# Feed-forward products by Strassen's scheme over 2x2 blocks, with the down product as a stage of its own

## The chip, the cores and the metric

The kernel runs on one core of a Trainium2 chip. A core has five engines with an instruction queue each: TensorE (PE in the profile, with its weight loads as PEld), VectorE (DVE), ScalarE (ACT), GpSimd (POOL) and SyncE (SP), which here issues most of the transfers between DRAM and the on-chip memory SBUF. Matrix products end in PSUM banks of 128 partitions by 512 fp32 values; there are eight of them. The metric is the time of one execution on the device in microseconds. The kernel before took 3261.09 us, the median of three runs (3260.57 to 3262.5).

## What is computed

One encoder block over 2048 tokens of width 1024, in fp32. The feed-forward part, which the change is about, has a hidden layer of 2816.

```
for l in range(DEPTH):                        # DEPTH = 1
    h = _rmsnorm(x, norm1_g[l])
    proj = h @ w_in[l]                        # 1024 -> 3264
    ...
    y_a = _hgrn2_group(...)                   # gated linear recurrence, both directions
    y_b = _mla_group(...)                     # latent attention, 4 heads
    x = x + jnp.concatenate([y_a, y_b], axis=-1) @ w_out[l]
    h = _rmsnorm(x, norm2_g[l])
    x = x + (jax.nn.silu(h @ w_gate[l]) * (h @ w_up[l])) @ w_down[l]   # 1024 -> 2816 -> 1024
return _rmsnorm(x, final_norm_g)
```

## The kernel before

Every product keeps fp32 accuracy by a split: an operand is cast to a rounded type on ScalarE (its high part, names ending in h), the rest is subtracted on VectorE or GpSimd (its low part, l), and three matmuls are added in PSUM, high by high, high by low and low by high. That is `mm3`, the lines 192 to 194. So a 128x512 piece of a product over 128 rows of the inner dimension costs three matmuls.

Phases 1 to 3 (input projection with the recurrence, latent projections, attention) are the same in both kernels. Phase 4, the output projection, goes over 16 token tiles of 128: products by `w_out`, the residual, a store of the result to DRAM (`x2_d`), and in `norm2_tile` the second norm, transposed by TensorE and moved out of PSUM. For the first eight tiles it is split in place; for the others it is stored in DRAM (`h2_d`).

Phase 5, the feed-forward part, goes over two halves of 1024 tokens (`hf`) and in each over 22 hidden tiles of 128 (`f`). Per hidden tile: `gate_up` for two blocks of 512 tokens (`bb`), 8 inner tiles x 3 matmuls for gate and as many for up, 96 in all. Then `s`, ScalarE's silu of the gate bank times the up bank on VectorE (L1121), and its split `th` (L1123, ScalarE) and `tl` (L1125, VectorE). `down` multiplies them by one 128x1024 tile of `w_down`, 8 token tiles x 2 column halves x 3 matmuls, 48, and VectorE adds each bank to the accumulator `acc` (L1088). So a hidden tile has 144 matmuls, and the eight banks are four for gate and up and four for down. The weights (`gr`, `ur`, `dr`) are loaded by SP a hidden tile ahead, cast by ScalarE (L989) and their low part is made by GpSimd (L991). At the change of half `h2_load` brings in the other 1024 tokens (L1062, L1063), and the first eight token tiles get their final norm: a sum of squares, a chain of some twelve VectorE operations on one column (`rstd_of`, names `rf_`), and the scaling by the row norm and the gain `gfin` (L1098 on VectorE, L1101 and L1102 on ScalarE and GpSimd). At the end the last two hidden tiles are taken together.

The order of each engine's queue is worked out when the program is built, from the data dependences and the buffers of each pool. So the order of the rows below says what stands behind what on an engine, and not when it runs.

## Time and profile before

| | |
|---|---|
| time, median of 3 runs | 3261.09 us (3260.57 to 3262.5) |
| span of the profiled execution | 3256.8 us (4.3 us below that median) |
| TensorE busy | 3134.8 us, 96%, 17169 matmuls recorded |
| VectorE busy | 1880.0 us, 58% |
| ScalarE busy | 1089.6 us, 33% |
| GpSimd busy | 689.7 us, 21% |
| output projection, inner stretch | 1580 to 1772 us |
| feed-forward part, first to last matmul | 1762.4 to 3245.3 us |

The profile is of one execution. Busy time of TensorE counts overlapping matmuls once, so that it can be near 100% while the engine is not at its best pace. The table by stretches gives the busy time of each engine between two moments, and the granted clock of TensorE in that stretch as a share of its full speed.

### The profile page before, as it was taken

To read this page: it belongs to the slowest core of one execution; us is meant where nothing else is said; L and a number is where in the kernel's file an instruction comes from. 1 tells how busy PE (TensorE), PEld (TensorE's weight loads), DVE (VectorE), ACT (ScalarE), POOL (GpSimd) and SP (SyncE) were. 2 spreads that over 40 slices of the span, in tenths; PEclk is the share of its full clock that TensorE was granted. 3 is DMA by queue.
4 is the path that set the end of the run, shared out by engine and by line. 5 is a ranking of instruction groups with operands and counts; after the bars stand their busy time and mean duration, and the time that the engine had idled before them with its cause. 6 is when DMAs were issued, how large, how long until landed. Compare 5 with 4: busy or idle time off the path is not lost.

```text
span 3256.8 us, 44545 instructions
## 1 busy us (share of the span) xinstructions
PE 3134.8 (96%) x17169; PEld 2628.2 (81%) x17169; DVE 1880.0 (58%) x4276; ACT 1089.6 (33%) x2037; POOL 689.7 (21%) x600
## 2 busy tenths in 40 slices
PE   7999999998989999999999999999999999999998
PEld 6999777776778888888888887888887788787877
DVE  6126558777768888888886434343436543434344
ACT  5101466665225555555432211111114111111112
POOL 1100233232241212110011322222222222212221
...
GB/s 172 71 63 56 64 67 79 75 88 123 198 189 34 40 32 46 24 25 24 167 142 192 87 46 47 45 52 45 52 46 138 107 47 46 46 46 52 46 39 52
DMA packets 231012, 245.00 MB, mean 75 GB/s; under 512 B 13416, under 2 KB 181904, under 8 KB 230800
## 3 DMA queue, kind: packets, MB, share of 16 engines
...
q10 hardware_dynamic: 1088, 2.90, 0.3%
...
q14 instruction: 77, 0.63, 0.1%
...
## 4 chain that ended last, share of the span: by engine, by line
PE 65%; DVE 10%; DMA 1%; issue 1%; ACT 1%; POOL 0%; SPq 0%; DVEq 0%; ACTq 0%; POOLq 0%
PE pu L194 5%; PE pg L193 5%; PE pu L193 5%; PE pu L192 5%; PE pg L192 5%; PE pg L194 5%; PE pd L192 3%; PE t L884 3%; PE pd L193 3%; PE pd L194 3%; DVE acc L1088 3%; DVE tl L1125 2%; PE s L847 2%; PE s L848 2%; PE o L193 2%; PE o L194 2%
## 5 line engine op out<-in xcount | busy, mean ns | idle before, releaser
L1121 DVE TENSOR_TENSOR s<-s,pu 128x512 f32<-128x512 f32 x88 | 60.5, 688 | 791.5 <-PE pu L194 791.5
L1088 DVE TENSOR_TENSOR acc<-acc,pd 128x512 f32<-128x512 f32 x688 | 429.4, 677 | 3.3 <-PE pd L194 3.0
L192 PE MATMUL pd<-dh,th 128*128 128x512 f32 x704 | 280.0, 398 | 29.9 <-DVE acc L1088 27.2
L193 PE MATMUL pd<-dl,th 128*128 128x512 f32 x704 | 275.1, 391 | 0.0
L194 PE MATMUL pd<-dh,tl 128*128 128x512 f32 x704 | 274.9, 391 | 0.0
L192 PE MATMUL pu<-h2h,uh 128*128 128x512 f32 x704 | 274.1, 389 | 0.0
L194 PE MATMUL pu<-h2h,ul 128*128 128x512 f32 x704 | 273.9, 389 | 0.0
L194 PE MATMUL pg<-h2h,gl 128*128 128x512 f32 x704 | 273.9, 389 | 0.0
L193 PE MATMUL pu<-h2l,uh 128*128 128x512 f32 x704 | 273.9, 389 | 0.0
L192 PE MATMUL pg<-h2h,gh 128*128 128x512 f32 x704 | 273.9, 389 | 0.0
L193 PE MATMUL pg<-h2l,gh 128*128 128x512 f32 x704 | 273.9, 389 | 0.0
L197 ACT ACTIVATE pth<-t 128x512 fp32r<-128x512 f32 x256 | 153.8, 603 | 248.0 <-PE t L884 248.0
L991 POOL TENSOR_TENSOR gl<-gr,gh 128x1024 fp32r<-128x1024 f32 x44 | 105.2, 2392 | 573.7 <-ACT gh L989 545.0
L858 DVE TENSOR_REDUCE mx<-s 128x1 f32<-128x512 f32 x256 | 175.3, 686 | 54.8 <-PE s L851 54.8
L991 POOL TENSOR_TENSOR dl<-dr,dh 128x1024 fp32r<-128x1024 f32 x44 | 105.6, 2400 | 423.5 <-ACT dh L989 387.5
L192 PEld LDWEIGHTS pd<-dh,th 128*128 128x128 f32 x704 | 132.5, 188 | 76.8 <-DVE acc L1088 48.9
L989 ACT ACTIVATE dh<-dr 128x1024 fp32r<-128x1024 f32 x44 | 46.7, 1062 | 419.3 <-PE pd L194 413.5
L867 ACT ACTIVATE pr<-s,nb 128x512 f32<-128x512 f32 x256 | 172.8, 688 | 14.9 <-DVE nb L861 11.1
L198 DVE TENSOR_TENSOR ptl<-t,pth 128x512 fp32r<-128x512 f32 x256 | 175.0, 685 | 2.2 <-ACT pth L197 0.5
L192 PE MATMUL o<-pth,vh 128*128 128x256 f32 x512 | 164.2, 321 | 0.3 <-DVE nb L861 0.3
L884 PE MATMUL t<-ident,pr 128*128 128x128 f32 x1024 | 153.2, 272 | 4.3 <-DVE pr L874 3.0
L884 PEld LDWEIGHTS t<-ident,pr 128*128 128x128 f32 x1024 | 125.5, 139 | 37.6 <-issue 1.7
...
## 6 DMA issues: line engine op xcount, KB each, us to landing
...
```

Of the source, the lines that this page charges most:

```text
L192: PE.matmul(ps, a_hi, b_hi, start=first, stop=False)
L193: PE.matmul(ps, a_hi, b_lo, start=False, stop=False)
L194: PE.matmul(ps, a_lo, b_hi, start=False, stop=last)
L197: ACT.activation(hi, ps, AF.Copy)
L198: DVE.tensor_tensor(lo, ps, fr(hi), op=ALU.subtract)
L847: PE.matmul(ps, q_hi[:, qs], k_hi, start=True, stop=False)
L848: PE.matmul(ps, q_hi[:, qs], k_lo, start=False, stop=False)
L858: last_mx[0] = DVE.tensor_reduce(mx[:, b:b + 1], ps, op=ALU.max, axis=AX.X)
L867: ACT.activation(PR[i][:, b, :], SB[i][b], AF.Exp, scale=SCALE, bias=nb, accum_out=rs[:, b:b + 1])
L884: PE.transpose(ps[:, j, :], PR[i][:, b, j * P:(j + 1) * P], ident)
L991: POOL.tensor_tensor(wl, raw, fr(wh), op=ALU.subtract)
L1088: DVE.tensor_add(acc[t][:, ns], acc[t][:, ns], banks[i, n])
```

## The change

The three products of the feed-forward part are made with Strassen's scheme (Winograd's form) over 2x2 blocks: seven products of quarter blocks instead of eight, and additions around them. The seven products are called P1 to P7. For an operand in blocks A11, A12, A21, A22 and weights B11 to B22:

```
S1 = A21+A22  S2 = S1-A11   S3 = A11-A21  S4 = A12-S2
T1 = B12-B11  T2 = B22-T1   T3 = B22-B12  T4' = B21-T2
P1 = A11 B11  P2 = A12 B21  P3 = S4 B22   P4 = A22 T4'  P5 = S1 T1  P6 = S2 T2  P7 = S3 T3
U2 = P1+P6    U3 = P1+P6+P7
C11 = P1+P2   C12 = U2+P5+P3   C21 = U3+P4   C22 = U3+P5
```

For gate and up the two weight matrices stand side by side: the columns 1 are gate, the columns 2 up, the rows 1 and 2 the upper and lower 512 of the inner dimension; the rows of A are two blocks of 512 tokens. A group is one hidden tile of one half of the tokens, 44 groups, in the order of `seq`; each has 7 products of 4 inner tiles x 3 matmuls, 84. P1 and P2 share a PSUM bank (a), P6, P7 and P4 another (b), P5 and P3 a third (c), and a bank is read between the products that go into it. The products of neighbouring groups are interleaved (`prods`, with an offset in groups).

What it adds and moves, part by part:

- *Output projection.* `norm2_tile` no longer splits; it keeps the transposed tiles (`hs`), makes S1 to S4 on GpSimd for every second block of four tiles and stores all seven operands to DRAM.
- *First operands.* `op_load` loads an operand in four pieces through eight raw buffers, casts on ScalarE, makes the low part on VectorE.
- *Gate and up.* `r_load` loads four quarter weights a group ahead, `t_make` makes T1 to T4 on GpSimd, `b_make` casts and makes the low part five products ahead, on VectorE for P2 and P4 and on GpSimd for the others. `after` adds up and multiplies on VectorE, makes the four sums of the down operand there and stores seven operands to DRAM (`g_d`).
- *Change of half.* In the last group of the first half each product is followed by the load of its operand for the second half.
- *Down.* It begins when gate and up are done for all tokens. Six passes P1, P2, P6, P7, P4, P5 have 11 steps of one pair of hidden tiles each, with 8 banks (8 token tiles) x 3 matmuls, 24 a step. A step's operand is loaded from DRAM and split (`g_op`), and its weights are loaded, summed on GpSimd and split (`w_op`: the T sums are made again here, up to three operations on GpSimd, with six raw buffers `wr`), two steps ahead. The banks are added into `t1`, `c11`, `U2` and `U3` after a pass; the residual comes in through `x2r` and a GpSimd addition after P6 and P7. P3 goes over token tiles (`last_g`), 33 matmuls each, so that the final norm of one lies beside the products of the next.

The diff, cut to its core:

```diff
@@ mm3
+    def mm3(ps, a_hi, a_lo, b_hi, b_lo, first, last, more=False):
@@ phase 4 and gate and up
+    OPS = ("A11", "S2", "A12", "S1", "S3", "A22", "S4")
+    def op_load(hf, i, pl):
+        hi, lo = (pl.tile([P, 4, 512], F32R, tag=f"{i}{c}", name=f"{i}{c}_{hf}") for c in "hl")
+        for j in range(4):
+            raw = fwr.tile([P, 512], F32, tag="raw", name=f"opr_{hf}_{i}_{j}", bufs=8)
+            SP.dma_start(out=raw, in_=h2_d[hf][i][:, j, :])
+            ACT.activation(hi[:, j, :], raw, AF.Copy)
+            DVE.tensor_tensor(lo[:, j, :], raw, fr(hi[:, j, :]), op=ALU.subtract)
+        op[i] = (hi, lo)
+    prods = (("P1", 0), ("P4", 1), ("P6", 0), ("P3", 1), ("P2", 0), ("P5", 0), ("P7", 0))
+    def t_make(n):
+        for nm, a, b in (("T1", "B12", "B11"), ("T2", "B22", "T1"), ("T3", "B22", "B12"), ("T4", "B21", "T2")):
...
+            POOL.tensor_tensor(R[nm, n], R[a, n], R[b, n], op=ALU.subtract)
+    def b_make(m):
...
+        pl, tag, bufs = (fwr, "u", 3) if m % 7 < 3 else (fwB, "v", 4)
+        hi, lo = (pl.tile([P, 4, P], F32R, tag=f"{tag}{c}", name=f"{nm}{c}_{n}", bufs=bufs) for c in "hl")
+        ACT.activation(hi, raw, AF.Copy)
+        eng = DVE if pr in ("P2", "P4") else POOL
+        eng.tensor_tensor(lo, raw, fr(hi), op=ALU.subtract)
+    def product(m):
+        if AHEAD > 0:
+            b_make(m + AHEAD)
...
+        for k in range(4):
+            mm3(ps, bh[:, k, :], bl[:, k, :], ah[:, k, :], al[:, k, :], new and k == 0, k == 3, not new)
...
+        if n == NF - 1:
+            op_load(1, A_OF[pr], opA if A_OF[pr] in ("A11", "S2") else fwB)
@@ norm2_tile
+                POOL.tensor_tensor(s1, a21, a22, op=ALU.add)
+                SP.dma_start(out=d["S1"][:, :, o], in_=s1)
+                POOL.tensor_tensor(a21, a11, a21, op=ALU.subtract)
...
@@ after P4
+            DVE.tensor_add(t1, t1, bank["b", n])
+            ACT.activation(t1, t1, AF.Silu)
+            g = G[2, up] = tmp("g", f"2_{n}", 6)
+            DVE.tensor_mul(g, t1, M["U3", n])
@@ down
+    def wd(nm, fp):
...
+        raw = fs.tile([P, 512], F32, tag="wr", name=f"{nm}d", bufs=6)
+        SP.dma_start(out=raw, in_=w_down[0, f * P:(f + 1) * P, n * 512:n * 512 + 512])
+    def w_op(pr, fp, pl, tag, bufs):
...
+        elif nm == "T4":
+            POOL.tensor_tensor(raw, raw, parts_[1], op=ALU.subtract)
+            POOL.tensor_tensor(raw, raw, parts_[2], op=ALU.add)
+            POOL.tensor_tensor(raw, raw, parts_[3], op=ALU.subtract)
...
+        ACT.activation(hi, raw, AF.Copy)
+        DVE.tensor_tensor(lo, raw, fr(hi), op=ALU.subtract)
+    def residual(dst, i, h, n):
+        raw = fd.tile([P, 512], F32, tag="x2r", name=f"x2r_{i}_{h}{n}", bufs=3)
...
+        POOL.tensor_tensor(dst, dst, raw, op=ALU.add)
+    dn = [(pr, fp) for pr in ("P1", "P2", "P6", "P7", "P4", "P5") for fp in range(NP)]
+    for m, (pr, fp) in enumerate(dn):
+        d_make(m + 2)
...
+            mm3(banks[i], th[:, o], tl[:, o], wh, wl, new and fp == 0, fp == NP - 1, not new)
+            if fp == NP - 1:
+                down_after(pr, i, banks[i])
+    LW = [w_op("P3", fp, lw, f"l{fp}", 1) for fp in range(NP)]
...
+            raw = fs.tile([P, NP, P], F32, tag="lr", name=f"lr_{i}", bufs=2)
+            SP.dma_start(out=raw, in_=g_d["S4"][:, :, i * P:(i + 1) * P])
...
-    def down(hf, f0, f1, tiles):
-        banks = {(i, n): bank4(f"pd_{hf}_{f1}_{i}_{n}", "x") for i in tiles for n in range(2)}
...
-                mm3(ps, th[:, o], tl[:, o], wh[:, ns], wl[:, ns], f == f0, f == f1)
...
-                DVE.tensor_add(acc[t][:, ns], acc[t][:, ns], banks[i, n])
```

Three places of the built programs show what stands behind what. The first is TensorE's queue, in the middle of the feed-forward part. Before, where the up product of hidden tile 18 (`pu_0_18_1`) ends and its down product (`pd`, by token tile and column half) begins:

```order
L192 MATMUL pu_0_18_1_22687<-h2h1_17259,uh_0_18_22507 128x512
L193 MATMUL pu_0_18_1_22687<-h2l1_17260,uh_0_18_22507 128x512
L194 MATMUL pu_0_18_1_22687<-h2h1_17259,ul_0_18_22509 128x512
L192 MATMUL pd_0_18_0_0_22727<-dh_0_18_22511,th_0_18_0_22654 128x512
L193 MATMUL pd_0_18_0_0_22727<-dl_0_18_22513,th_0_18_0_22654 128x512
L194 MATMUL pd_0_18_0_0_22727<-dh_0_18_22511,tl_0_18_0_22656 128x512
L192 MATMUL pd_0_18_0_1_22728<-dh_0_18_22511,th_0_18_0_22654 128x512
L193 MATMUL pd_0_18_0_1_22728<-dl_0_18_22513,th_0_18_0_22654 128x512
L194 MATMUL pd_0_18_0_1_22728<-dh_0_18_22511,tl_0_18_0_22656 128x512
```

Now, where P4 of group 1 (operand A22, weights T4, bank `pb_1`) is followed by P6 of group 2 (operand S2, weights T2, bank `pb_2`):

```order
L193 MATMUL pb_1_19175<-A22h_0_18992,T4h_1_19190 128x512
L194 MATMUL pb_1_19175<-A22l_0_18993,T4h_1_19190 128x512
L195 MATMUL pb_1_19175<-A22h_0_18992,T4l_1_19191 128x512
L193 MATMUL pb_2_19323<-S2h_0_18441,T2h_2_19210 128x512
L194 MATMUL pb_2_19323<-S2l_0_18442,T2h_2_19210 128x512
L195 MATMUL pb_2_19323<-S2h_0_18441,T2l_2_19211 128x512
```

The shape of a matmul is the same, 128x512; the down product has left this part, and the products of neighbouring groups alternate. TensorE's list has 14738 rows before and 13946 now, 792 fewer.

The second is GpSimd's queue. Before, in the second half, it holds the low parts of the weights of hidden tiles 10 and 11 and nothing else:

```order
L991 TENSOR_TENSOR gl_1_10_25659<-gr_1_10_25594,gh_1_10_25657 128x1024
L991 TENSOR_TENSOR ul_1_10_25720<-ur_1_10_25596,uh_1_10_25718 128x1024
L991 TENSOR_TENSOR dl_1_10_25724<-dr_1_10_25598,dh_1_10_25722 128x1024
L991 TENSOR_TENSOR gl_1_11_25871<-gr_1_11_25806,gh_1_11_25869 128x1024
L991 TENSOR_TENSOR ul_1_11_25932<-ur_1_11_25808,uh_1_11_25930 128x1024
```

Now, at the passage from P7 to P4 of the down stage, the sums of T4 (`B21d`, three operations for each step) and the residual additions that follow P7 (L1245, into `U3d` and `t1d`):

```order
L1220 TENSOR_TENSOR B21d_27800<-B21d_27800,B11d_27806 128x512
L1245 TENSOR_TENSOR U3d_0_27664<-U3d_0_27664,x2r_0_11_27666 128x512
L1245 TENSOR_TENSOR t1d_0_26247<-t1d_0_26247,x2r_0_10_27669 128x512
L1218 TENSOR_TENSOR B21d_27845<-B21d_27845,B22d_27847 128x512
L1219 TENSOR_TENSOR B21d_27845<-B21d_27845,B12d_27849 128x512
L1245 TENSOR_TENSOR U3d_1_27675<-U3d_1_27675,x2r_1_11_27677 128x512
L1245 TENSOR_TENSOR t1d_1_26254<-t1d_1_26254,x2r_1_10_27680 128x512
L1245 TENSOR_TENSOR U3d_2_27686<-U3d_2_27686,x2r_2_11_27688 128x512
L1245 TENSOR_TENSOR t1d_2_26261<-t1d_2_26261,x2r_2_10_27691 128x512
L1245 TENSOR_TENSOR U3d_3_27697<-U3d_3_27697,x2r_3_11_27699 128x512
L1245 TENSOR_TENSOR t1d_3_26268<-t1d_3_26268,x2r_3_10_27702 128x512
L1220 TENSOR_TENSOR B21d_27845<-B21d_27845,B11d_27851 128x512
```

The sums of the fifth step of P4 (`B21d_27845`) stand among the 16 residual additions, of which eight more follow before the sixth step's sums.

The third is VectorE's queue. Before, in the middle of the first half: the silu products `s`, the low parts `tl` and the additions that clear the banks of `down`:

```order
L1088 TENSOR_TENSOR acc_7_18827<-acc_7_18827,pd_0_7_7_1_20466 128x512
L1121 TENSOR_TENSOR s_0_8_0_20531<-s_0_8_0_20531,pu_0_8_0_20506 128x512
L1125 TENSOR_TENSOR tl_0_8_0_20536<-s_0_8_0_20531,th_0_8_0_20534 128x512
L1121 TENSOR_TENSOR s_0_8_1_20592<-s_0_8_1_20592,pu_0_8_1_20567 128x512
L1088 TENSOR_TENSOR acc_0_18813<-acc_0_18813,pd_0_8_0_0_20607 128x512
L1088 TENSOR_TENSOR acc_0_18813<-acc_0_18813,pd_0_8_0_1_20608 128x512
L1125 TENSOR_TENSOR tl_0_8_1_20597<-s_0_8_1_20592,th_0_8_1_20595 128x512
```

Now, at the passage from P5 to P3, among the row norms of the token tiles that P5 finishes (`rf_13` to `rf_15`, one column each; L1262 is the scaling), the low parts of the first two operands of P3 (`lgl_0` and `lgl_1`, L1332):

```order
L1262 SCALAR_TENSOR_TENSOR t1d_5_26282<-t1d_5_26282,rf_13_r_28781,gfin_25838 128x512
L177 SCALAR_TENSOR_TENSOR rf_14_t_28807<-rf_14_r_28806,rf_14_a_28804 128x1
L184 TENSOR_TENSOR rf_15_r_28831<-rf_15_r_28831,rf_15_t_28832 128x1
L1332 TENSOR_TENSOR lgl_0_28920<-lr_0_28917,lgh_0_28919 128x1408
L186 TENSOR_SCALAR rf_14_a_28804<-rf_14_t_28807 128x1
L177 SCALAR_TENSOR_TENSOR rf_15_t_28832<-rf_15_r_28831,rf_15_a_28829 128x1
L187 TENSOR_TENSOR rf_14_t_28807<-rf_14_a_28804,rf_14_t_28807 128x1
L186 TENSOR_SCALAR rf_15_a_28829<-rf_15_t_28832 128x1
L1332 TENSOR_TENSOR lgl_1_28926<-lr_1_28923,lgh_1_28925 128x1408
```

`lgl_0`, on which the first matmul group of P3 waits, stands behind the row norms and most of the scalings of eight token tiles.

## Rows read from the trace of the kernel before

**Rows 1.** The page: span, busy time, GB/s in 40 slices, chain's shares.

```profile
span 3256.8 us, 44545 instructions
PE 3134.8 (96%) x17169; PEld 2628.2 (81%) x17169; DVE 1880.0 (58%) x4276; ACT 1089.6 (33%) x2037; POOL 689.7 (21%) x600
...
GB/s 172 71 63 56 64 67 79 75 88 123 198 189 34 40 32 46 24 25 24 167 142 192 87 46 47 45 52 45 52 46 138 107 47 46 46 46 52 46 39 52
...
PE 65%; DVE 10%; DMA 1%; issue 1%; ACT 1%; POOL 0%; SPq 0%; DVEq 0%; ACTq 0%; POOLq 0%
```

**Rows 2.** Stretches: length, busy PE PEld DVE ACT POOL, clock, DMA share, GB/s.

```profile
1550.00:1580.00 30.00, 27.29 (x175) 23.51 (x174) 25.84 (x58) 18.94 (x37) 2.54 (x4) 1.00 0.77 240
1580.00:1772.00 192.00, 190.56 (x914) 157.53 (x913) 153.60 (x470) 65.81 (x143) 21.65 (x30) 1.00 0.43 140
1819.00:2488.00 669.00, 658.61 (x2881) 538.70 (x2880) 278.46 (x405) 111.28 (x143) 141.13 (x59) 1.00 0.16 50
2488.00:2535.00 47.00, 37.36 (x156) 28.56 (x155) 45.54 (x124) 26.53 (x53) 21.61 (x12) 0.96 0.70 226
```

**Rows 3.** Timeline of PE: start, duration, what ended the idle time before.

```profile
2149.71 0.39 PE L192 MATMUL pu<-h2h,uh 128*128 128x512 f32 x1
...
2152.43 0.39 PE L192 MATMUL pd<-dh,th 128*128 128x512 f32 x1
...
2157.19 0.50 PE L192 MATMUL pd<-dh,th 128*128 128x512 f32 x1 [0.52 <-DVE acc L1088]
```

**Rows 4.** The chain that ended last: start, time on it, what.

```profile
1852.15 1.29 DVE acc L1088 x2
...
2454.54 1.29 DVE acc L1088 x2
...
2487.25 0.69 DVE s L1121
...
2566.03 0.69 DVE s L1121
```

**Rows 5.** First feed-forward matmuls (groups by tile), the last, the end (timeline).

```profile
L192 PE MATMUL pg<-h2h,gh x704: 387/389/397, 1762.4 to 3228.1; 128*128 128x512 f32 x176
...
3244.90 0.39 PE L194 MATMUL pd<-dh,tl 128*128 128x512 f32 x1
...
3251.99 1.41 DVE L1098 SCALAR_TENSOR_TENSOR acc<-acc,rf_r,gfin 128x512 f32<-128x512 f32 x2
```

**Rows 6.** Groups of instructions (busy us, mean ns); one from the timeline.

```profile
L1088 DVE TENSOR_TENSOR acc<-acc,pd 128x512 f32<-128x512 f32 x688 | 429.4, 677 | 3.3 <-PE pd L194 3.0
...
L639 POOL TENSOR_TENSOR kl<-kraw,kh 128x512 fp32r<-128x512 f32 x16 | 20.8, 1300 | 8.9 <-DVE kh L638 3.2 <-issue 3.1 <-ACT kns L205 1.7
...
L989 ACT ACTIVATE dh<-dr 128x1024 fp32r<-128x1024 f32 x44 | 46.7, 1062 | 419.3 <-PE pd L194 413.5 <-DMA dr<-in_w_down_dram 5.5 <-POOL acc L1102 0.3
...
L1123 ACT ACTIVATE th<-s 128x512 fp32r<-128x512 f32 x88 | 55.6, 632 | 245.7 <-DVE s L1121 245.7
...
2494.80 1.22 DVE L1063 TENSOR_TENSOR h2l<-h2r,h2h 128x1024 fp32r<-128x1024 f32 x1 [0.39 <-ACT h2h L1062]
```

**Rows 7.** Timeline of VectorE beside GpSimd.

```profile
2143.21 0.69 DVE L1125 TENSOR_TENSOR tl<-s,th 128x512 fp32r<-128x512 f32 x1 [0.70 <-ACT th L1123]
...
2153.31 1.37 DVE L1088 TENSOR_TENSOR acc<-acc,pd 128x512 f32<-128x512 f32 x2
2153.59 2.39 POOL L991 TENSOR_TENSOR ul<-ur,uh 128x1024 fp32r<-128x1024 f32 x1 [3.05 <-ACT uh L989]
2154.60 1.94 DVE L1125 TENSOR_TENSOR tl<-s,th 128x512 fp32r<-128x512 f32 x1
```

**Rows 8.** DMA issues of the page: times, KB each, median us to landing.

```profile
wr_r<-in_w_in_dram SPq DMA_DIRECT2D x24, 256.0 KB, 3.0
```

**Rows 9.** Timeline of VectorE: first and last norm scaling at the change of half.

```profile
2504.32 0.74 DVE L1098 SCALAR_TENSOR_TENSOR acc<-acc,rf_r,gfin 128x512 f32<-128x512 f32 x1
...
2529.23 3.46 DVE L1098 SCALAR_TENSOR_TENSOR acc<-acc,rf_r,gfin 128x512 f32<-128x512 f32 x2
```

376 lines of the change are left out of this document (245 added, 131 removed).

## The prediction

> **What bounds the kernel now.** The page comes first: TensorE is busy for 96% of the span, and 65% of the chain that ended last is PE [rows 1]. Busy is not yet pace, so next comes the table by stretches: in the feed-forward part (1762 to 3245 us) PE is idle for about 10 of the first half's 669 us, VectorE is busy for 42%, GpSimd for 21%, DMA for a sixth [rows 2]. So PE's instruction count sets this part, and the price of one matmul is wanted. The mean of one (389 ns) is a latency, since matmuls overlap; the pace is read from starts: twelve starts lie 2.72 us apart, 0.2267 us for one of 512 columns [rows 3]. The part holds 9 groups of 704, so 6336 matmuls or 1436.4 us; it runs from 1762.4 to 3245.3 us, 1482.9 us [rows 5]. The other 46.5 us are two things. Each hidden tile takes 33.47 us on the chain (602.4 us for 18 of them) where its 144 matmuls need 32.64; the 0.8 us is PE waiting for VectorE to clear a bank of the down product [rows 3, 4]. And the change of half costs 78.8 us for two tiles instead of 66.9, 11.9 us [rows 4].
>
> **The change: matmuls.** Seven quarter products replace eight. Gate and up: 44 hidden tiles of 7 x 12 matmuls instead of 96, 3696 for 4224. Down: 66 steps of 24 and 8 x 33 at the end, 1848 for 2112. That is 5544, 792 fewer; the built programs differ by just that number of PE rows. The shape stays 128x128 against 128x512, so I keep 0.2267 us: 1256.8 us, a group of 84 in 19.04 us and a step of the down stage in 5.44 us. If all that waits stayed, 179.6 us are saved. What remains is to price the new waits that take the place of the old 46.5 us.
>
> **The side engines in the gate and up stage.** Per group of 19.04 us GpSimd makes four sums and five low parts, 9 x 1.30 = 11.7 us [rows 6]. VectorE has five adds from PSUM at 0.68 (3.4 us) and on average six operations with two SBUF inputs (two low parts, two products, half of the four sums), 6 x 0.69 = 4.1 us. ScalarE casts seven times and evacuates three times, 10 x 0.63 = 6.3 us. Each fits. But two of them do not run side by side: a low part on VectorE that takes 0.69 us alone took 1.94 us while GpSimd worked from 2153.59 to 2155.98, and ended 0.56 us after it, while two adds from PSUM at the same moment took 1.37 us together [rows 7]. So an operation of VectorE with two SBUF inputs waits for the end of GpSimd's, and the two columns add: 11.7 + 4.1 = 15.8 of 19.04 us. It fits, at 83%. The Trainium skill says the same (SBUF — State Buffer, "SBUF: two separate sides"): the port pair that the two engines share is an exclusive lock for a whole instruction, not a split of bandwidth. By that rule the change would be priced by the sum of both engines and not by the larger, and the trace agrees, 1.94 against 0.69 us.
>
> The one tight bank is b: between its sum P7 and its next use P4 there is one product, 2.72 us, and the add that clears it needs about 1.3 us after the last matmul (0.39 + 0.1 + 0.69 + 0.1); a VectorE operation held by GpSimd ahead of it (up to 1.3 + 0.69) uses the rest. Between 0 and 0.4 us per group; I take 0.1, **4 us** (0 to 18).
>
> **The output projection** (1580 to 1772 us, PE 190.6 of 192 us busy, VectorE 80% [rows 2]) gets four GpSimd sums of 1.3 us in 8 of its 16 tiles of 12 us, and seven stores per pair of tiles, where before had none in the first half and four in the second. The sums can hold VectorE by up to 1.3 us each: none if the slack of 20% takes it, 15 us if half of the 8 x 5.2 us shows through less the evacuations saved. I take **4 us** (0 to 15); the stores stay behind a queue with a tile of lead.
>
> **First operands.** After two products five operands (20 loads, casts and low parts) have to come through eight raw buffers, at 0.69 to 1.3 us each for VectorE, 14 to 26 us. PE has the products of A11 and S2 for two groups first (10.9 us), and the order puts S1 and A12 next as they come. Between 0 and 15 us, I take **6**.
>
> **The change of half.** All seven operands are replaced: 28 low parts of 0.69, on top of two groups: 19.3 + 8.3 + 23.4 = 51 us of VectorE with two inputs and GpSimd, within 38.1 us and the lead of five products (13.6 us). That just fits on paper, and VectorE's adds stand behind the low parts in its queue. The nearest row is the present change of half, 11.9 us [rows 4]. From 3 to 25 us; I take **10**.
>
> **The passage to the down stage** is covered: its first operands are loaded among the last products, and five of its matmuls stand before them on PE. **2 us** (0 to 8).
>
> **Steps of the down stage.** Each 5.44 us needs a cast of 1.06 and of 0.63 us and low parts of 1.22 and about 0.69 us [rows 6]. P1, P2: no GpSimd. P7, P5: one sum, 1.3 + 1.9 = 3.2 us of the pair. P6: two, 4.5 us. **3 us** for these (0 to 10). P4 is another matter: three sums, 3.9 + 1.9 = 5.8 us against 5.44. And its weights come through six buffers, four to a step, so one of the four loads waits until VectorE has made the low part of the step before. That closes a loop: load 3.0 us [rows 8], two sums 2.6, ScalarE's cast 0.63, a wait for GpSimd's next sum 0.6, the low part 0.69, handovers about 0.4: 7.9 us per step. At its front stand the 16 residual adds of P7 (20.8 us on GpSimd), among them the sums of the fifth step. Its weights are there about 29 us after P7 ends, where PE wants them at 27.2; five more steps at 7.9 against 5.44 add 12.3. So **14 us** (4, if loads land at once, to 30, if a load takes 4.5 us: 1.5 for each of eleven steps).
>
> **The passage to P3.** Its first group needs the low part lgl_0, which stands on VectorE behind the row norms of eight tiles. Counted by instruction they leave it about 16 us after the last matmul of P5; the eight norms at the present change of half took 28 us, from 2504.3 to 2532.7 [rows 9], with larger GpSimd work between. TensorE stood still for 10 us there and was granted 0.96 of its clock over 47 us, so a piece at the lower level of 1.2 GHz for 1.9 us lost [rows 2]. **18 us** (12 to 28), clock included.
>
> **The end.** From the last matmul to the end of the span are 11.5 us today [rows 5]; after the change one tile's half is left, the add, square, row norm, two scalings and the store: about 8.2 us. Gain **3.3**.
>
> **Sum.** New waits 4 + 4 + 6 + 10 + 2 + 3 + 14 + 18 = 61 us. 1256.8 + 61 = 1317.8 for 1482.9: 165.1 less, with the end 168.4. The profiled span of 3256.8 becomes 3088.4. The median of the runs, 3261.09, lies 4.3 us above that span, for what lies around it: **3092.7, so 3092 us**, 5.2% less.
>
> **Rivals.**
> - *The order covers nearly all.* All lows together (0, 0, 0, 3, 0, 0, 4, 12) are 19 us, which gives 3050; with up to 40 us of waits 3071. For it: the sums of work fit everywhere but in P4. Against: VectorE stood held by GpSimd in every hidden tile of before.
> - *The pair of VectorE and GpSimd sets the gate and up stage.* At 83% of a group, handovers of 0.3 us at each of 15 operations fill it; 1.5 us per group over it is 66 us: 3159 (3121 to 3200). The Trainium skill's rule of the shared port (SBUF — State Buffer, "SBUF: two separate sides"), taken strictly, leans to this side. Against it: GpSimd runs five products ahead.
> - *The down stage is fed too slowly.* P4 moves 1.57 MB per step, 289 GB/s; 240 GB/s was reached at a DMA share of 0.77 [rows 2]. At the 192 GB/s of the page's second busiest slice [rows 1], P4's steps would take 8.2 us and P6's 6.8: 46 us instead of the 14, 3125.
> - *Slower than before.* The same pair, in every group: the mean group at 22.9 us instead of 19.04 eats 44 x 3.85 = 169 us, and from there the kernel is slower. It would need GpSimd's operations to cost 1.7 us each in the row; nothing in the trace shows this between 128x512 operations (1.30 the mean of 16 [rows 6]).
> - That fewer matmuls are not what is saved can't be: they are gone from PE's list.
>
> **Chances.** Waits of 40 to 90 us, 3071 to 3121, my forecast: 0.50. The order covers it, 3050 to 3071: 0.22. The pair sets the stage, 3121 to 3200: 0.18. Slow feed, about 3125: 0.07. Slower: 0.03. A measurement of this kernel tells 0.2% from no change (6.5 us). All but the last lie beyond it on the fast side: faster 0.96, slower 0.03, within 0.01. From 3055 to 3145 leaves out the fastest fifth of the second case, half of the third and the last, 0.15 to 0.2.
>
> **What would show it.** Right: PE's pace still 0.227 us; groups of 19.0 to 19.3 us in the gate and up stage; an idle time of 12 to 28 us ahead of P3, ended by lgl_0 on VectorE; P4's eleven steps some 14 us longer than P2's, PE waiting there for VectorE's low part of the weights. Wrong: groups above 20 us with PE waiting on low parts or bank clears, a matmul pace other than 0.227, or DMA at its limit in P4 and P6.

## The result, and the profile after

The changed kernel takes 3155.09 us (median of four runs, 3151.73 to 3157.26) where the kernel before takes 3260.83 us on the same chips (3258.79 to 3262.5): a ratio of 0.9677, with an interval of 0.9663 to 0.9691. It is faster by 105.7 us. I had forecast 168.4 us less, 3092 us with a range of 3055 to 3145. The direction holds, and fewer matmuls are what is gained; what the change loses elsewhere is twice what I priced.

The page of the changed kernel, with the parts that answer to [rows 1]:

```profile
span 3151.7 us, 45387 instructions
...
PE 2993.7 (95%) x16377; PEld 2498.4 (79%) x16377; DVE 1972.6 (63%) x4138; ACT 1258.3 (40%) x2365; POOL 1138.9 (36%) x998
...
PE 58%; DMA 7%; DVE 6%; POOL 4%; issue 2%; ACT 1%; SPq 0%; POOLq 0%; DVEq 0%; ACTq 0%
```

TensorE still looks full (95%), but DMA and GpSimd, 1% and 0% of the chain before, are now 7% and 4% of it: the side work has come onto the path. The table by stretches (length, busy PE PEld DVE ACT POOL, clock, DMA share, GB/s) says where:

```profile
1580.00:1772.00 192.00, 178.48 (x819) 144.86 (x818) 159.49 (x444) 62.56 (x138) 60.35 (x59) 0.96 0.60 191
1850.93:2181.07 330.14, 330.14 (x1429) 268.37 (x1428) 180.86 (x185) 102.47 (x170) 228.74 (x158) 1.00 0.33 104
2670.00:2730.00 60.00, 60.00 (x266) 49.64 (x266) 25.11 (x32) 19.41 (x26) 0.00 (x0) 1.00 0.72 242
2908.00:2970.00 62.00, 43.19 (x163) 33.53 (x162) 26.28 (x21) 10.87 (x13) 49.90 (x34) 0.84 0.72 235
3030.00:3080.00 50.00, 33.11 (x140) 25.72 (x138) 34.94 (x115) 23.49 (x41) 11.37 (x8) 0.86 0.59 194
```

The first line is the output projection: TensorE is idle for 13.5 of 192 us where it was idle for 1.4 [rows 2], and its granted clock is 0.96 where it was 1.00, which costs some 7 us more (0.04 of 192). The second is 17 groups of gate and up: never idle, and still 330.14 us where 17 x 19.04 us is 323.7. The third is P1 of the down stage, at its full pace. The fourth is the passage from P7 to P4 with P4's first steps, and the fifth the one from P5 to P3, with 19 and 17 us idle. The timeline of TensorE at these places:

```profile
1725.72 0.59 PE L818 MATMUL ysum<-ones,y 128*128 128x2 f32 x2 [5.48 <-POOL y L810]
...
1794.96 1.30 PE L1057 MATMUL h2T<-ident,xn 128*128 128x128 f32 x5 [6.77 <-DVE xn L1050]
...
1909.19 0.40 PE L193 MATMUL pa<-A11h,B11h 128*128 128x512 f32 x1
...
1928.61 0.40 PE L193 MATMUL pa<-A11h,B11h 128*128 128x512 f32 x1
...
2229.06 0.79 PE L193 MATMUL pb<-A22h,T4h 128*128 128x512 f32 x1 [6.17 <-DVE U L1147]
...
2854.01 0.80 PE L193 MATMUL pd_P<-dh_P,gh_P 128*128 128x512 f32 x1 [3.92 <-DVE U2d L1282]
2854.61 0.63 PE L194 MATMUL pd_P<-dl_P,gh_P 128*128 128x512 f32 x1
2855.04 0.63 PE L195 MATMUL pd_P<-dh_P,gl_P 128*128 128x512 f32 x1
...
2923.11 0.80 PE L193 MATMUL pd_P<-dh_P,gh_P 128*128 128x512 f32 x1 [4.85 <-DVE U3d L1286]
...
2965.56 0.79 PE L193 MATMUL pd_P<-dh_P,gh_P 128*128 128x512 f32 x1 [8.14 <-ACT dh_P L1222]
...
3070.20 0.80 PE L193 MATMUL pd_P<-dh_P,lgh 128*128 128x512 f32 x1 [6.86 <-ACT lgh L1331]
...
3080.23 0.79 PE L195 MATMUL pd_P<-dh_P,lgl 128*128 128x512 f32 x1 [8.81 <-DVE rf_a L186]
...
3142.88 0.39 PE L195 MATMUL pd_P<-dh_P,lgl 128*128 128x512 f32 x1
```

Two group starts lie 19.42 us apart, not 19.04, with no gap between. After the waits of 3.92 and 4.85 us the starts are 0.43 us apart for eight to ten matmuls, the lower clock level of 1.2 GHz (granted 0.84 from 2908 to 2970 us), so that each of these waits costs 2 us more than its idle time. The wait at 2229.06, at the change of half, ends with VectorE's add that clears bank b (L1147), and in VectorE's queue that add stands behind a low part of the new operand S2:

```profile
2227.72 0.69 DVE L971 TENSOR_TENSOR S2l<-opr_S,S2h 128x512 fp32r<-128x512 f32 x1 [1.90 <-ACT S2h L970]
2228.32 0.68 DVE L1147 TENSOR_TENSOR U<-t,pb 128x512 f32<-128x512 f32 x1
```

Groups by tile (min/median/max ns, first and last start):

```profile
L193 PE MATMUL pa<-A11h,B11h x176: 387/396/774, 1782.5 to 2645.7; 128*128 128x512 f32 x176
...
L193 PE MATMUL pd_P<-dh_P,gh_P x528: 387/389/797, 2663.0 to 3062.5; 128*128 128x512 f32 x176
```

Gate and up begin at 1782.5 instead of 1762.4 [rows 5]. The down stage's six passes run from 2663.0 to 3062.95, 399.9 us; their 66 steps of 5.44 us with 24 matmuls left over from gate and up need 364.5. Groups by form (busy us, mean ns, idle before and what ended it):

```profile
L1057 PE MATMUL h2T<-ident,xn 128*128 128x128 f32 x128 | 22.4, 306 | 14.2 <-DVE xn L1050 11.9 <-DVE ry_a L169 2.3
...
L818 PE MATMUL ysum<-ones,y 128*128 128x2 f32 x32 | 5.3, 234 | 6.8 <-POOL y L810 6.5
...
L193 PE MATMUL pd_P<-dh_P,gh_P 128*128 128x512 f32 x528 | 208.7, 397 | 23.2 <-ACT dh_P L1222 11.8 <-DVE U3d L1286 6.8 <-DVE U2d L1282 4.7
...
L1014 DVE TENSOR_TENSOR T4l<-T,T4h 128x512 fp32r<-128x512 f32 x44 | 47.6, 1081 | 1.9 <-ACT T4h L1012 1.9
...
L1014 POOL TENSOR_TENSOR B22l<-B22r,B22h 128x512 fp32r<-128x512 f32 x44 | 69.9, 1588 | 7.7 <-ACT B22h L1012 7.7
```

By the terms of the prediction, in us (where TensorE loses time against 0.2267 us a matmul):

| term | predicted | measured |
|---|---|---|
| output projection | 4 (0 to 15) | 20.1 (1782.5 for 1762.4) |
| first operands | 6 (0 to 15) | 15.7 (228 matmuls at 0.2312 us, 52.7, took 68.4: 1782.54 to 1850.93) |
| bank b in the other groups | 4 (0 to 18) | 0 |
| pace of the gate and up matmuls | 0 | 16.7 (44 x 0.38) |
| change of half | 10 (3 to 25) | 15.9 (four groups in 93.6 for 77.7) |
| passage up to down | 2 (0 to 8) | 0.2 |
| steps of P1, P2, P6, P7, P5 | 3 (0 to 10) | 18.4: ends of P6 and P7 7.1 and 8.9, P5 2.4 |
| P4 | 14 (4 to 30) | 17.0 |
| passage to P3 | 18 (12 to 28) | 18.1 |
| pace of P3 | 0 | 2.0 |
| sum | 61 | 124.1 |

The end after the last matmul is 8.8 us, for 8.2. The sum is 63.1 us over mine, the span 63.3.

### The profile page after: what moved, and what is told of

The parts are those of the page before. It is cut to its first block, busy times and chain, and to the rows that moved or that the text cites. A ratio compares the mean times of both kernels' runs of the same rounds, so it can differ in the third digit from the quotient of the medians.

```text
span 3151.7 us, 45387 instructions
## 1 busy us (share of the span) xinstructions
PE 2993.7 (95%) x16377; PEld 2498.4 (79%) x16377; DVE 1972.6 (63%) x4138; ACT 1258.3 (40%) x2365; POOL 1138.9 (36%) x998
## 4 chain that ended last, share of the span: by engine, by line
PE 58%; DMA 7%; DVE 6%; POOL 4%; issue 2%; ACT 1%; SPq 0%; POOLq 0%; DVEq 0%; ACTq 0%
PE pb L193 4%; PE pb L194 4%; PE pb L195 3%; PE t L885 3%; PE pc L195 2%; PE pc L194 2%; PE pc L193 2%; PE pa L193 2%; PE pa L194 2%; PE pa L195 2%; PE pd_P L195 2%; PE pd_P L194 2%; PE pd_P L193 2%; PE s L852 2%; PE s L850 2%
## 5 line engine op out<-in xcount | busy, mean ns | idle before, releaser
L193 PE MATMUL pd_P<-dh_P,gh_P 128*128 128x512 f32 x528 | 208.7, 397 | 23.2 <-ACT dh_P L1222 11.8
L194 PE MATMUL pd_P<-dl_P,gh_P 128*128 128x512 f32 x528 | 208.9, 396 | 1.7 <-DVE dl_P L1223 1.7
L195 PE MATMUL pd_P<-dh_P,gl_P 128*128 128x512 f32 x528 | 207.9, 394 | 0.0
L1232 DVE TENSOR_TENSOR gl_P<-gr_P,gh_P 128x1024 fp32r<-128x1024 f32 x66 | 95.0, 1439 | 169.5 <-ACT gh_P L1231 167.8
L195 PE MATMUL o<-pth,vl 128*128 128x256 f32 x512 | 143.9, 281 | 0.0
L194 PE MATMUL o<-ptl,vh 128*128 128x256 f32 x512 | 143.8, 281 | 0.0
L193 PEld LDWEIGHTS pd_P<-dh_P,gh_P 128*128 128x128 f32 x528 | 100.9, 191 | 47.5 <-ACT dh_P L1222 13.0
L875 DVE TENSOR_SCALAR pr<-pr,ri 128x512 f32<-128x512 f32 x256 | 127.3, 511 | 2.2
L194 PEld LDWEIGHTS pd_P<-dl_P,gh_P 128*128 128x128 f32 x528 | 100.9, 191 | 24.2 <-DVE dl_P L1223 3.2
L195 PEld LDWEIGHTS pd_P<-dh_P,gl_P 128*128 128x128 f32 x528 | 100.9, 191 | 21.1
L1147 DVE TENSOR_TENSOR U<-t,pb 128x512 f32<-128x512 f32 x44 | 30.2, 686 | 125.0 <-PE pb L195 125.0
```

The costliest lines, as they stand in the source:

```text
L193: PE.matmul(ps, a_hi, b_hi, start=first, stop=False, skip_group_check=more)
L194: PE.matmul(ps, a_hi, b_lo, start=False, stop=False, skip_group_check=more)
L195: PE.matmul(ps, a_lo, b_hi, start=False, stop=last, skip_group_check=more)
L875: DVE.tensor_scalar(PR[i][:, b, :], PR[i][:, b, :], ri, None, op0=ALU.mult)
L1232: DVE.tensor_tensor(lo, raw, fr(hi), op=ALU.subtract)
```

## The experiments

Times are medians, each beside the kernel before on the same chip. "The changed kernel" is 3155.1 us, 0.9677 of it.

### The pace of the matmuls

My first suspicion was the place of the operands in SBUF: the two operands of one matmul lie in pools on the left side (opA, `u`) or the right side (fwB, `v`), and their start addresses differ by product. Five kernels move one side by a tile that nobody uses.

```diff
+    rim = ctx.enter_context(pool("rim", side="right"))
+    rim.tile([P, 8], F32, tag="rim", name="rim")
     fwB = es_g.enter_context(pool("fwB", side="right"))
```

That is **e1_align**. **e9_same2048** and **e10_off256** have 488 and 424 elements in place of 8, and **e3_allodd** puts the 8 ahead of opA on the left. **e2_before_shift** does it to the kernel before, in which the two operands begin alike:

```diff
+    rim = ctx.enter_context(pool("rim"))
+    rim.tile([P, 8], F32, tag="rim", name="rim")
     h2p = ctx.enter_context(pool("h2"))
+    rim2 = ctx.enter_context(pool("rim2"))
+    rim2.tile([P, 24], F32, tag="rim2", name="rim2")
     fwr = ctx.enter_context(pool("fwr"))
```

> The changed kernel with 32 unused bytes per partition at the upper end of SBUF, so that the operands of the gate and up stage and of P3 that lie there begin at a multiple of 64 bytes, as those at the lower end do. Theory offset: a matmul whose two operands begin at different offsets within 64 bytes starts every 0.2343 us and not 0.2267; then a group of gate and up takes 19.04 us and not 19.42, P3 runs at 0.2267, and the time falls by 44 x 0.38 + 264 x 0.0076 = 18.7 us to about 3136 us. Rival: the slower pace comes from the side engines, GpSimd above all, which is busy for 70% of the stage; then nothing changes, 3155 us.

> The kernel before, with the moving operand of gate and up (the transposed tokens) put 32 bytes further, everything else at its old offset within 128 bytes. Theory offset: the 4224 matmuls of gate and up start every 0.2343 us and not 0.2267, 32 us more, about 3293 us; the down products keep 0.2267. Rival (side engines): no change, 3261 us.

> The changed kernel with 32 unused bytes at the lower end, so that all operands of gate and up begin 32 bytes past a multiple of 64; P3 stays as it was. Theory offset, in the form that only a difference between the two operands costs: groups of 19.04 us, P3 at 0.2343, about 3138 us. In the other form, that an operand past a multiple of 64 costs by itself: every product at 2.81 us, groups of 19.7 us, about 3166 us. Side engines: 3155 us.

> The changed kernel with 1952 unused bytes at the upper end, so that every operand of gate and up and of P3, on either side of SBUF, begins at the same offset within 512 bytes (64). In the two runs before, the operands of either side still differed by 128 bytes, and the pairs that cross sides still ran at 0.233. Theory offset, now: a pair of operands costs nothing only if both begin at the same offset within 512 bytes (or 256); then all seven products take 2.72 us, a group 19.04, P3 runs at 0.2267, and the time falls by 18.7 us to about 3136. Rival, that the pairs across sides are slow for their place and not for the offset: groups stay at 19.3 us, about 3152.

> The same with 1696 bytes, so that operands of the two sides differ by 256 bytes within 512. If the offset counts within 256 bytes, the products across sides (A11, A12 and S4) take 2.72 us; if it counts within 512, they take 2.79 or more. Rival (place of the pair): 2.79 to 2.82.

Measured, with where the operands of each side begin within 256 bytes (from the built programs; P3's stationary operand begins at 64 in all the changed ones):

```
kernel            left / right     a group    P3 of down   time us   ratio (interval)
changed             64 / 224        19.42       0.2343      3155.1   0.9677 (0.9663 to 0.9691)
e1_align            64 / 192        19.33       0.2324      3153.3   0.9671 (0.9653 to 0.9689)
e3_allodd           96 / 224        19.33       0.2343      3151.7   0.9672 (0.9658 to 0.9687)
e9_same2048         64 /  64        19.04       0.2267      3139.2   0.9636 (0.9621 to 0.965)
e10_off256          64 /  64        19.04       0.2267      3138.9   (one run)
e2_before_shift   96 apart (gate and up)        0.234       3291.0   1.0098 (1.0083 to 1.0113)
```

e1 missed (3136 was expected): I had taken 64 bytes for the unit, and its sides still differed by 128. e10 makes them alike within 256 bytes and not within 512, and does as well as e9. e2 does the reverse: its edit puts 32 bytes ahead of the moving operand and 32 + 96 ahead of the stationary one, which I had taken for no shift at all, so the two are 96 apart. The kernel before loses the 31 us that its 4224 matmuls at 0.234 us make. Timelines of TensorE, of e9 two starts of a group and of e2 two starts twelve matmuls apart:

```profile
1891.23 0.39 PE L193 MATMUL pa<-A11h,B11h 128*128 128x512 f32 x1
...
1910.27 0.39 PE L193 MATMUL pa<-A11h,B11h 128*128 128x512 f32 x1
```

```profile
2004.23 0.40 PE L192 MATMUL pg<-h2h,gh 128*128 128x512 f32 x1
...
2007.04 0.40 PE L192 MATMUL pg<-h2h,gh 128*128 128x512 f32 x1
```

19.04 and 2.81 us, where the changed kernel and the kernel before have 19.42 and 2.72. The side engines are no rival: in e9 GpSimd is as busy (stretch, columns as above), and the pace is the full one.

```profile
1853.15:2170.00 316.85, 316.85 (x1399) 262.39 (x1398) 172.86 (x184) 100.82 (x167) 217.38 (x152) 1.00 0.33 106
```

In the changed kernel the products with operands on different sides (A11, S4, A12) take 2.81 to 2.82 us, those on one side (S1, S3, S2, A22) 2.72 to 2.77; what the latter lose lies in their first four to nine matmuls, behind a product with operands on other sides, and their last ones start 0.227 us apart. So the pace is lost where the moving and the stationary operand begin at different offsets within 256 bytes; 16 us hang on it.

### The output projection

**e7_nosums** leaves the sums S1 to S4 out and stores the blocks as they are (that part of the computation is missing); **e6_start** keeps GpSimd's T sums for group 1 behind the last squares of `y`.

```diff
-                POOL.tensor_tensor(s1, a21, a22, op=ALU.add)
+                s1 = a22
-                POOL.tensor_tensor(a21, a11, a21, op=ALU.subtract)
-                POOL.tensor_tensor(a11, s1, a11, op=ALU.subtract)
-                POOL.tensor_tensor(a12, a12, a11, op=ALU.subtract)
```

> The changed kernel without the four GpSimd sums S1 to S4 in the output projection (tiles are stored as they are, so the operands are others). Theory of the prediction, that these sums hold VectorE: the first product of gate and up, at 1782.5 us with the sums and at 1762.4 before the change, comes 4 to 8 us earlier, 3147 to 3151 us. Rival: the 20 us come from the sums of weights of the next group, which stand ahead of the squares of the attention rows in GpSimd's queue; then it comes at most 2 us earlier, and the wait of TensorE for those squares of 5.5 us at 1720 us stays.

```diff
-            t_make(n)
+            with tc.issue_after(YP[-1].ins):  # n == 1; YP: GpSimd's sums of squares of y
+                t_make(n)
```

> The changed kernel with one thing moved: GpSimd's sums of weights for the second group stand behind the squares of the last token tile in its queue. Theory: TensorE's wait for those squares at 1720 us (5.5 us, and 1.7 us at the lower clock level) goes, 6 to 8 us less, about 3148. Rival: the wait moves to another place of the output projection, where VectorE is late, or to the first operands; 3153 to 3155.

e7: 3134.5 us, 0.9624 (0.9606 to 0.9641), 20.6 less. e6: 3154.0 us, 0.9678 (0.9662 to 0.9694), nothing. Groups by form, of e7 and then of e6:

```profile
L1057 PE MATMUL h2T<-ident,xn 128*128 128x128 f32 x128 | 20.5, 287 | 8.6 <-DVE xn L1050 6.3 <-DVE ry_a L169 2.2
...
L818 PE MATMUL ysum<-ones,y 128*128 128x2 f32 x32 | 4.6, 214 | 0.7 <-POOL y L810 0.7
```

```profile
L1062 PE MATMUL h2T<-ident,xn 128*128 128x128 f32 x128 | 21.0, 293 | 19.7 <-DVE xn L1055 17.1 <-DVE ry_a L169 2.6
...
L818 PE MATMUL ysum<-ones,y 128*128 128x2 f32 x32 | 5.1, 228 | 2.8 <-POOL y L810 2.5
```

In the changed kernel GpSimd stands at a T sum whose weights come late, with the squares of `y` behind it (its timeline):

```profile
1721.11 1.26 POOL L997 TENSOR_TENSOR T<-B22r,T 128x512 f32<-128x512 f32 x1 [5.08 <-DMA B22r<-in_w_up_dram]
...
1724.23 1.43 POOL L810 TENSOR_TENSOR y<-y 128x128 f32<-128x128 f32 x1
```

e6 takes that wait away (6.5 to 2.5 us), and the transposes wait 5.2 us longer for VectorE's `xn`: the order of GpSimd's queue moves the loss and doesn't cause it. Without the sums both waits shrink, by 5.8 and 5.6 us. So the sums on GpSimd cost some 14 us ahead of gate and up (first product at 1768.6) and about 6 us behind it; the other 6 of the 20 us ahead of it no run explains. The sums do hold VectorE, as the prediction had it: a scaled low part of `y`, with two SBUF inputs, takes 0.50 us with them and 0.34 without. By form, of the changed kernel and of e7:

```profile
L814 DVE SCALAR_TENSOR_TENSOR yl<-y,gcols,yh 128x128 fp32r<-128x128 f32 x64 | 30.3, 499 | 0.0
```

```profile
L814 DVE SCALAR_TENSOR_TENSOR yl<-y,gcols,yh 128x128 fp32r<-128x128 f32 x64 | 20.1, 342 | 0.0
```

How much of the 14 us is this hold and how much a queue that was put together otherwise, e7 doesn't part.

### The down stage

Rival causes of its 35 us: the order on VectorE, where at the end of a pass low parts for the next steps stand ahead of the adds that clear the banks (**e4_passages** puts them behind); too few buffers for loads (**e8_rings**); the 16 residual additions ahead of P4 (**e8_resid** spreads them, two to a step); the loads themselves (**e13_noloads** makes the sums of one loaded tile with itself instead of up to four tiles); GpSimd's sums (**e14_nosums_down** leaves them out). The last two miss that part of the computation. **e16_t4early** makes the T4 sums of P4 during P1 and P2, where GpSimd has nothing to do, and keeps them in eleven tiles.

```diff
-            DVE.tensor_tensor(lo, raw, fr(hi), op=ALU.subtract)
+            hold.append((lo, raw, hi))          # last step of P6, P7, P4
...
+            with tc.issue_after(adds[-1].ins):  # the eighth bank's add
+                for lo, raw, hi in hold:
+                    DVE.tensor_tensor(lo, raw, fr(hi), op=ALU.subtract)
```

> The changed kernel with one thing moved in the down stage: where P6, P7 and P4 end, the low parts of the step after next are put on VectorE behind the eight additions that read the banks, and not behind the first of them. Theory: TensorE's waits there for these additions (U2d, U3d: 1.1 + 4.3 us and 2.3 + 5.3 us, and some 3.5 us at the lower clock level behind them) are the low parts that wait for a transfer; they go, 10 to 14 us less, about 3143. Rival: the additions are held by GpSimd's sums; then the waits stay, 3155.

```diff
-        raw = fs.tile([P, 512], F32, tag="wr", name=f"{nm}d", bufs=6)
+        raw = fs.tile([P, 512], F32, tag="wr", name=f"{nm}d", bufs=12)
...
-        raw = fd.tile([P, 512], F32, tag="x2r", name=f"x2r_{i}_{h}{n}", bufs=3)
+        raw = fd.tile([P, 512], F32, tag="x2r", name=f"x2r_{i}_{h}{n}", bufs=8)
```

> The changed kernel with 12 buffers and not 6 for the quarter weights of the down stage, and 8 and not 3 for the residual. TensorE waits 34 us in the six passes of the down stage (399 us for 66 steps of 5.44 and 24 matmuls of the stage before). Theory of the prediction, a loop through too few buffers with the residual additions at its front: most of it goes, 24 to 28 us less, about 3129. Rival, that the transfers themselves are too slow (289 GB/s asked for in P4): at most 6 us less, 3149 or more, with P4 at about 8 us a step.

```diff
-            residual(u3, i, 1, 1)
-            residual(t1, i, 1, 0)
+            late.append((i, u3, t1))
...
+        if pr == "P4" and fp > 0 and late:
+            i, u3, t1 = late.pop(0)
+            residual(u3, i, 1, 1)
+            residual(t1, i, 1, 0)
```

> The changed kernel with its few buffers, and one thing moved: the 16 residual additions that follow P7 are spread over the steps of P4, two to a step, behind the sums of that step's weights. If the residuals at the front make P4 late, P4's 17 us of waits fall to 6 or less, about 3144; if the loop through the six buffers does, they stay, now spread over P4's steps, 3153 or more.

```diff
-        parts_ = [wd(b, fp) for b in SUMS.get(nm, (nm,))]
+        parts_ = [wd(SUMS.get(nm, (nm,))[0], fp)] * len(SUMS.get(nm, (nm,)))
```

> The changed kernel, in whose down stage a sum of weights takes the same loaded tile for all its terms: one load of weights a step and not up to four, the GpSimd operations as before (the weights of P4 to P7 and P3 are others). If the transfers make the down stage wait, its 34 us of waits in the six passes fall below 10, about 3128; if GpSimd's operations do, they stay above 25, 3147 or more.

```diff
-        raw = parts_[0]
+        raw, nm = parts_[0], "none"
```

> The changed kernel, in whose down stage the sums of weights are left out on GpSimd, the loads as before (the weights of P4 to P7 are the first of their terms). If GpSimd's sums make the down stage wait, the 34 us fall below 12, about 3130; if the transfers do, they stay above 25, 3147 or more.

```diff
+        parts_ = [T4[fp]] if nm == "T4" else [wd(b, fp) for b in SUMS.get(nm, (nm,))]
...
+        if 2 <= m < 2 * NP + 2 and m % 2 == 0:
+            t4_make((m - 2) // 2)
```

> The changed kernel with the sums of P4's weights made and kept in SBUF from the third step of P1 on, where GpSimd is idle, so that P4 has neither sums nor weight loads of its own. If P4's own sums and loads cause its 17 us of waits and the 9 us at the end of P7, some 20 us go, about 3135; if the transfers of the whole down stage do, the waits move into P1, P2 and P6, 3150 or more.

Measured: e4 3159.0 us, 0.9696 (0.968 to 0.9713), no gain. e8_rings 3186.7 us, 0.9778 (0.9761 to 0.9794), 31 worse. e8_resid 3152.4 us, 0.9673 (0.9654 to 0.9693). e13 and e14, one run each, 3119.4 and 3125.4 us. e16 3140.4 us, 0.9634 (0.9618 to 0.965), 15 less. Timeline of TensorE in e4:

```profile
2851.83 0.47 PE L193 MATMUL pd_P<-dh_P,gh_P 128*128 128x512 f32 x1 [2.31 <-DVE U2d L1288]
...
2881.43 0.79 PE L193 MATMUL pd_P<-dh_P,gh_P 128*128 128x512 f32 x1 [5.99 <-ACT dh_P L1222]
```

The wait for the bank's add falls from 3.92 to 2.31 us, and later steps wait for ScalarE's cast of the weights (5.99 us, and 9.49 us at 2955.31): the supply is late, and the order on VectorE only says where that shows. SyncE's and ScalarE's timelines of e4 show one link of it:

```profile
2870.49 4.80 SPq L1250 DMA_DIRECT2D x2r<-s_x  x4
...
2879.80 1.06 ACT L1234 ACTIVATE gh_P<-gr_P 128x1024 fp32r<-128x1024 f32 x1 [13.88 <-DMA gr_P<-s_gS]
```

The load of the step's operand (`gr_P`) is issued at 2875.38, behind four loads of the residual, which wait for GpSimd's additions to free their three buffers; ScalarE is idle for 13.88 us until it lands. In the changed kernel, too, SyncE's residual loads wait 17 us for GpSimd between 2930 and 2966 us. No run moves these loads without the additions. Timeline of TensorE in e8_rings, and in two steps of P4 in e8_resid:

```profile
2680.76 1.65 PE L193 MATMUL pd_P<-dh_P,gh_P 128*128 128x512 f32 x3 [11.02 <-ACT dh_P L1222]
```

```profile
2966.29 0.51 PE L193 MATMUL pd_P<-dh_P,gh_P 128*128 128x512 f32 x1 [0.41 <-ACT dh_P L1222]
...
2974.16 0.49 PE L193 MATMUL pd_P<-dh_P,gh_P 128*128 128x512 f32 x1 [1.24 <-ACT dh_P L1222]
```

With larger rings SyncE's queue is put together otherwise. The first load of the stage is issued 16 us later, behind the last stores of gate and up, and the stage begins with a wait of 11 us, 17.7 us later in all; P7 and P5 lose more too. So this run says little of the rings themselves. SyncE's first load, of the changed kernel and of e8_rings:

```profile
2657.14 0.32 SPq L1229 DMA_DIRECT2D gr_P<-s_gA  x1
```

```profile
2673.44 0.42 SPq L1229 DMA_DIRECT2D gr_P<-s_gA  x1
```

With the residual additions spread, P4's long wait of 8.14 us is gone (the one at its front, for U3d, stays with 4.18), but five of its steps take 7.4 to 8.1 us instead of 5.44; the two rows are 7.87 apart, with a wait at each. The loss goes from one place to several. 7.87 is what I had worked out for P4's loop, but here it is GpSimd that is full, with three sums and two additions a step: 38.03 of 40 us (stretch of e8_resid, columns as above).

```profile
2950.00:2990.00 40.00, 32.79 (x123) 24.61 (x122) 16.77 (x12) 8.89 (x12) 38.03 (x25) 0.91 0.86 286
```

The first of the three matmuls of each product in the six passes (groups by form), of e13, e14 and e16:

```profile
L193 PE MATMUL pd_P<-dh_P,gh_P 128*128 128x512 f32 x528 | 204.8, 389 | 0.0
```

```profile
L193 PE MATMUL pd_P<-dh_P,gh_P 128*128 128x512 f32 x528 | 205.5, 390 | 1.2 <-ACT dh_P L1222 1.2
```

```profile
L193 PE MATMUL pd_P<-dh_P,gh_P 128*128 128x512 f32 x528 | 206.9, 393 | 14.9 <-DVE c11d L1274 7.2 <-DVE U2d L1278 6.2 <-DVE U3d L1282 1.6
```

Without the loads, with the sums: no wait, and every step takes 5.44 us. Without the sums, with all loads: 1.2 us, and with the waits of the other matmuls and the lower clock behind them some 6 of the 35 us. So neither the transfers nor GpSimd's sums alone make the stage late. What is left is the series load, sums, cast, low part, which has two steps of time; that it is this series is argued and not shown, since both runs also relieve the six weight buffers (one tile a step in e13, tiles that nothing reads in e14) and the queues around them. e16 cuts the series for P4 at its longest member, and the waits of P4 and P5 are gone; at the end of P6 one of 6.2 us stays, at the end of P7 it shrinks to 1.6 us, and the earlier sums bring a new one of 7.2 us at the end of P2.

### The passage to P3

**e5_norms** puts the row norms of P5's eight tiles behind P3's first two low parts.

```diff
-            finish(i, 1, C["t1", i], C["U3", i])
...
+        if i == 0:
+            with tc.issue_after(lows[1].ins):
+                for j in range(8):
+                    finish(j, 1, C["t1", j], C["U3", j])
```

> The changed kernel with one thing moved: the row norms of the eight token tiles that P5 finishes stand on VectorE behind the low parts of the first two operands of P3, and not ahead of them. Theory of the prediction: TensorE's two waits ahead of P3 (7.0 and 9.2 us, with 2 us at the lower clock level behind them) are these norms; some 4 us stay for the load and split of the first operand, so 12 to 14 us less, about 3142. Rival: the norms then hold up P3's next operands or the end, and less than 4 us is gained.

3147.6 us, 0.9655 (0.9639 to 0.9672), 7.5 less where 12 to 14 were expected. Timeline of TensorE:

```profile
3070.47 0.68 PE L193 MATMUL pd_P<-dh_P,lgh 128*128 128x512 f32 x1 [3.33 <-ACT lgh L1330]
...
3072.14 0.79 PE L195 MATMUL pd_P<-dh_P,lgl 128*128 128x512 f32 x1 [0.56 <-DVE lgl L1331]
```

The waits of 6.86 and 8.81 us become 3.33 and 0.56, and in the trace the passage is 9.7 us shorter, not 18.1: the load and split of the first operand stay, and the norms now run beside P3, where one later group waits 0.9 us for a row norm.

### Together

**e12_combo** has the edits of e10, e5 and e8_rings, **e15_best** those of e10 and e5, **e17_best2** those of e10, e5 and e16, and **e18_best3** those of e17 with e4's also at the end of P2.

> Three things together: operands at the same offset within 256 bytes (16 to 18.7 us), the row norms behind the first operands of P3 (13), and the larger rings of the down stage (25). If they are independent, 54 us less than the changed kernel, about 3101; if the down stage is bound by its transfers, 3125 to 3130.

> Operands at the same offset within 256 bytes, and the row norms behind the first operands of P3, nothing else: 16 us and 8 us less than the changed kernel as measured one by one, about 3131 us; if they are not independent, 3136 to 3140.

> Operands at the same offset within 256 bytes, the row norms behind the first operands of P3, and P4's sums made early. If independent, 16 + 8 + 15 = 39 us less than the changed kernel, about 3116; if the earlier pace only brings the waits for transfers nearer, 3122 to 3127.

> The same, and where P2, P6, P7 and P4 end, the low parts of the step after next stand on VectorE behind the eight additions. With the supply of P4 out of the way the waits for c11d, U2d and U3d (7.2, 6.2 and 1.6 us, some 5 us of lower clock behind them) should now go: 12 to 18 us less than e17, 3100 to 3104. Rival, that the supply is late anyway, as in e4: as e17, 3116.

e12: 3160.1 us, 0.9704 (0.9688 to 0.972), the three differences added (-16, -8, +31). e15: 3133.8 us, 0.9614 (0.9599 to 0.9628). **e17: 3116.6 us (3113.9 to 3122.8), 0.9567 (0.9552 to 0.9581), the fastest version, 38.5 us ahead of the changed kernel (36 by the ratios).** e18: 3123.2 us, 0.9585 (0.9569 to 0.9601), no gain over e17: 6.6 us more in the median, and the intervals overlap. Groups by form, of e17 and of e18:

```profile
L193 PE MATMUL pd_P<-dh_P,gh_P 128*128 128x512 f32 x528 | 208.4, 396 | 14.5 <-DVE c11d L1276 8.1 <-DVE U2d L1280 4.6 <-DVE U3d L1284 1.8
```

```profile
L193 PE MATMUL pd_P<-dh_P,gh_P 128*128 128x512 f32 x528 | 208.7, 396 | 8.2 <-ACT dh_P L1220 8.2
```

The waits for the adds disappear from e18, and waits for the cast come in their place, as in e4.

## Why the prediction was off

**What failed.** Three terms lie well outside what I gave them, and with any one of them as priced the time would have come out inside the range: the pace of the matmuls, put at no loss (18.7 us), the output projection (20.1 us for at most 15), and the passages between the passes of the down stage (16.0 of the 18.4 us for the steps, at most 10).

**Right.** 792 matmuls fewer are what is gained. The passage to P3 came out at 18.1 us for 18, its place as forecast, and the row norms as its cause (e5). Only the first of its two waits ends otherwise, with ScalarE's cast of the high part and not with the low part. Gate and up stay TensorE's: away from the two passages where operands are loaded, no group waits for a low part or for bank b. The end, the passage to the down stage and the steps of P1 and P2 hold.

**The pair of VectorE and GpSimd.** I priced a group by the sum of both engines, 15.8 of 19.04 us, and TensorE doesn't wait for them. The rival by which it sets the stage gives 3159 us, near the measured time, but by coincidence, since its mechanism isn't there: TensorE is never idle in those groups and gets the full pace in e9 with the same side work. The operations do hold each other up: the low part of T4 takes 1.08 us on VectorE where 0.69 is its time alone, and that of B22 takes 1.59 us on GpSimd where 1.30 was the mean before [rows 6]. The Trainium skill (SBUF — State Buffer, "SBUF: two separate sides") has the two engines lock their shared port for a whole instruction each; the trace agrees, on both engines' sides.

**"So I keep 0.2267 us"** (the matmuls) failed: the shape is the same, the addresses are not. It is 18.7 us of the 63, shown by e9, e10 and, backwards, e2. Why differing offsets cost this is open.

**"None if the slack of 20% takes it"** (the output projection) failed in size: 20.1 us for 4, above my bound of 15. That the sums hold VectorE was right, that its slack takes it was not. My reading is that busy shares don't price this stage, in which each tile is a chain across five engines: a row norm, transposes, evacuations. GpSimd's sums delay links of that chain, and slack elsewhere in the tile doesn't give it back. e7 shows that the sums are the cause of 14 of the 20 us, e6 that the one place in GpSimd's queue that I suspected is not; 6 us stay open.

**First operands** were mis-sized, 15.7 for 6, and by a wait that the term didn't hold: 6.77 us, its longest, are the last tile's transposes, which stand among the first products and wait for VectorE's second norm. The low parts and casts of the operands, which it did hold, stop TensorE for 2.5 us, the clear of bank b for 1.4, and the lower clock takes most of the rest. About 6 us go with the sums (e7).

**The change of half** (15.9 for 10, within its bounds) has the mechanism that I named: its waits of 6.17 and 2.42 us end with VectorE's add for bank b, which stands behind low parts of new operands whose loads come late; the operands themselves take 2.3 us, the lower clock some 5.

**The down stage.** I priced its steps one at a time, by a sum of engine times; the passages P6 to P7 and P7 to P4, where the banks are cleared and the next weights must come at once, I didn't price at all: 16.0 us. For P4, 17.0 us for 14, the size was right and the reason half wrong, so it was partly luck: the residual additions at its front are there, and GpSimd is full with them from 2932 to 2961 us, but my loop of 7.9 us a step isn't, since its steps from 2974 us on are 5.44 us apart. The slow feed isn't a matter of bandwidth alone: P1 runs at 242 GB/s without a wait, and e14 moves all the weights for some 6 us. What is left, by argument, is the length of the series behind each load.

**Open:** why the offsets of the operands cost pace; what share of the start the sums have as work and as order, and what the 6 us are that stay without them; in the down stage, the shares of the series, of the six weight buffers and of SyncE's order.
